# RWKV's key slabs and low-rank output slab: split beside three feed-forward output products instead of at the passage into RWKV, in a hybrid Mamba-2/RWKV-7 trunk on one Trainium2 core

## The chip, the core and the metric

The kernel runs on one core of one Trainium2 chip. The metric is the device time of one execution in microseconds (us); lower is better. The engines have these names in the rows: PE is TensorE's matrix multiply, PEld its weight load, DVE is VectorE, ACT is ScalarE, POOL is GpSimd, SP is SyncE, which here issues nearly all DMAs (SPq is its queue). The timeline counts microseconds from the start of the profiled span.

## The reference, cut to what matters

512 frames of 1024 features run through two layers. Each layer is feed-forward, mixer, feed-forward; the first mixer is a Mamba-2 scan, the second RWKV-7. All arrays are float32.

```python
def swiglu_ffn(x, w_in, w_out):
    gate, up = jnp.split(x @ w_in, 2, axis=-1)
    return (jax.nn.silu(gate) * up) @ w_out
...
def rwkv7_mixer(u, v_first, mix, w_rkv, w_o, w0, w1, w2, a0, a1, a2, g1, g2, ...):
    delta = jnp.pad(u, ((0, 0), (1, 0), (0, 0)))[:, :-1] - u
    shift = lambda idx: u + delta * mix[idx]
    r, k, v = shift(0) @ w_rkv[0], shift(2) @ w_rkv[1], shift(3) @ w_rkv[2]
    w_log = -softplus(-(w0 + jnp.tanh(shift(1) @ w1) @ w2)) - 0.5
    alpha = jax.nn.sigmoid(a0 + (shift(4) @ a1) @ a2)
    ...                                    # recurrence over frames, group norm, gate
    return (y * g) @ w_o, v

def reference(x, norms, ffn_w_in, ffn_w_out, ...):
    for i in range(2):
        t = swiglu_ffn(rmsnorm(h, norms[i, 0]), ffn_w_in[i, 0], ffn_w_out[i, 0])
        h = h + 0.5 * rmsnorm(t, norms[i, 1])
        u = rmsnorm(h, norms[i, 2])
        t = mamba2_mixer(u, ...) if i == 0 else rwkv7_mixer(u, ...)
        h = h + rmsnorm(t, norms[i, 3])
        t = swiglu_ffn(rmsnorm(h, norms[i, 4]), ffn_w_in[i, 1], ffn_w_out[i, 1])
        h = h + 0.5 * rmsnorm(t, norms[i, 5])
    return h
```

## The kernel before, in words

**Three products for one.** Every float32 matrix product is made of three passes on PE. A weight slab, 128 x 1024 floats (512 KB), is loaded into a tile `raw`; ACT casts it to a high part (`whi`, line 112), DVE or POOL subtracts that from the original to get the low part (`wlo`, line 113). Activations are split likewise: `hh`, `hl` for the hidden tiles of a feed-forward block, `xmh`, `xml` for RWKV's mixed inputs. `mm3` then multiplies high by high, high by low and low by high.

**The stream.** The class `Stream` numbers all weight slabs of the program in the order of their use and loads and splits them ahead of it. There are four `raw` buffers and eight buffers each for `whi` and `wlo`. `get()` hands out the next slab and prefetches; `pause_after` and `resume` stop and restart it. All loads go through SP's queue, in one order; an entry that has no free buffer holds up everything behind it.

**Kept slabs.** Some slabs of RWKV are loaded and split long before they are used. Their two parts are stored in DRAM (`khi_d`, `klo_d`, line 150) and later loaded as parts straight into `whi` and `wlo` (line 126), so that no engine splits them then. `Stream.store` is a generator: each step loads one such slab, splits it (always on DVE) and sends off the parts of the one before. The feed-forward blocks step it (`more`) beside their output products. Before, 16 slabs are kept: RWKV's eight r slabs and eight v slabs.

**The stages.** They are `ffn0`, `mamba`, `ffn1`, `ffn2`, `rwkv`, `ffn3`. Each ends in `out_phase`, which multiplies by the output weights: for a feed-forward block 22 slabs, one for each hidden tile k (`acc` banks). Up to k = 17 (k = 13 in `ffn2`) PE takes slab after slab; the rest is multiplied half by half of the frames, so that the norm of the first half can start. There a scheduler sets the order of the instructions of all engines from the program's order; from the tail on the order of ACT, DVE and POOL is that of the code.

**The passage from `ffn2` into `rwkv`.** The last eight output slabs are held in all eight buffers and multiplied half by half (`deep`). As the last of them end, the norm of the second half (`nb`), the mixing of RWKV's inputs (`xa`, `xb`) and the first products of the keys (`nxt.pair`, banks `pk`) are interleaved by a string of letters, run by `run`. `0`, `1`, `2` each multiply one k of a pair of heads (six matmuls); `x` and `y` mix one k of the first or second half; `N` and `n` step the norm; `e` and `z` square and scale the last bank; `s` and `t` split the next slab, `s` with its low part on DVE, `t` on POOL. The strings are `S0`, `S1` and `SEQ`. In this part the order on PE is that of the code, too.

Of the kernel before, what the change touches and what calls it, by code (L numbers as in the profile page):

```python
# [57 lines left out]
SQ = 8  # L58

S0 = "ttxxx"  # L60
S1 = "xxt"
SEQ = "s00ezN1x11NN10x110nxN00n0111222tt22NNx02x"

# [7 lines left out]
def step(g, n=1):  # L73
    for _ in range(n):
        next(g, None)


class Stream:
# [5 lines left out]
    def __init__(self, nc, raw, split, dram, aps, stored, own, ahead=6, split_ahead=4):  # L84
        self.nc, self.raw, self.split, self.aps, self.own = nc, raw, split, aps, own
        self.kept = {i: [dram.tile([P, SLAB], F32, tag=f"{z}{i}", name=f"{z}_d") for z in ("khi", "klo")]
                     for i in range(stored[0], stored[0] + stored[1])}
        self.loaded, self.parts = [], []
        self.pos = 0
        self.lo_eng = nc.vector  # L90
        self.ahead, self.split_ahead = ahead, split_ahead
        self.limit = len(aps)
        self.hold = False
# [42 lines left out]
    def store(self, first, n):  # L136

        made = None
        for i in list(self.kept)[first:first + n]:
            t = self._raw(i)  # L140
            if made:
                self._send(*made)
            made = i, self._parts(i, *t, self.nc.vector)
            yield
        self._send(*made)
        yield
# [25 lines left out]
    def get(self):  # L172
        i = self.pos
        self.pos += 1
        self.prefetch(i)
        return self.parts[i]
# [81 lines left out]
class Trunk:  # L258
    def __init__(self, ctx, tc, ins, out, plan=("ffn0", "mamba", "ffn1", "ffn2", "rwkv", "ffn3")):
        nc = self.nc = tc.nc  # L260
        self.tc, self.ins = tc, ins
        self.const = ctx.enter_context(tc.tile_pool(name="const", bufs=1))
        self.small = ctx.enter_context(tc.tile_pool(name="small", bufs=4))
        self.ps = ctx.enter_context(tc.tile_pool(name="ps", bufs=8, space=PSUM))
        self.dram = ctx.enter_context(tc.tile_pool(name="dram", bufs=1, space=DRAM))
        raw = ctx.enter_context(tc.tile_pool(name="raw", bufs=4))
        split = ctx.enter_context(tc.tile_pool(name="split", bufs=8))
        self.slots = ctx.enter_context(tc.tile_pool(name="slots", bufs=54))

        make = {"ffn": Ffn, "mam": Mamba, "rwk": Rwkv}  # L270
        gis = {"ffn0": 0, "mamba": 2, "ffn1": 4, "ffn2": 6, "rwkv": 8, "ffn3": 10}
        stages = [make[p[:3]](self, gis[p], 0.5 if p[0] == "f" else 1.0) for p in plan]
        slabs = [s.slabs() for s in stages]
        base = [sum(map(len, slabs[:i])) for i in range(len(plan))]
        own = set()
        for b, s in zip(base, stages):
            s.base = b
            own |= {b + i for i in s.own()}
        self.stream = Stream(nc, raw, split, self.dram, [ap for z in slabs for ap in z],
                             (base[plan.index("rwkv")] + 9, 16), own)  # L280

        self.h = [self.slot("h") for _ in range(KD)]
        x = ins["x"].rearrange("p (k t) -> p k t", k=KD)
        self.vec = self.const.tile([P, V_END], F32, tag="vec", name="vec")
        self.cst = self.const.tile([P, C_END], F32, tag="cst", name="cst")
        nc.scalar.dma_start(self.vec[:, :V_CW], ins["vec"][:, :V_CW])
        for hf in range(2):
            self.stream.load_ahead(hf + 1)
            for k in range(KD):
                nc.sync.dma_start(self.h[k][:, HALF[hf]], x[:, k, HALF[hf]])  # L290
        self.stream.load_ahead(4)
        nc.sync.dma_start(self.cst, ins["cst"])
        nc.sync.dma_start(self.vec[:, V_CW:], ins["vec"][:, V_CW:])
        self.ident = self.cst[:, C_ID:C_ID + P]
        self.ones = self.cst[:, C_ONE:C_ONE + P]
        self.tri = self.cst[:, C_TRI:C_TRI + P]

        self.fill = iter(())
        self.new_rs()
        first = stages[0]  # L300
        first.start()
        for i, st in enumerate(stages):
            st.body(stages[i + 1] if i + 1 < len(stages) else Output(self, out))
# [104 lines left out]
    def out_phase(self, get, nk, gi, scale, nxt, side=None, wide=False, eps=None, more=iter(())):  # L408
# [7 lines left out]
        nc = self.nc  # L416
# [33 lines left out]
        def mm(hf, m, k, w, x):  # L450
            c = cols(m, k)
            self.mm3(place[hf, m], [a[:, c] for a in w], [a[:, HALF[hf]] for a in x],
                     k == 0 and (hf, m // 2) in pairs and m % 2 == 0, k == nk - 1)

        def mm_all(m, k, w, x):
            c = cols(m, k)
            self.mm3(banks[m], [a[:, c] for a in w], x, k == 0, k == nk - 1)
# [6 lines left out]
        for k in range(nk):  # L464
            if deep and k == nk - tail:
                self.stream.pause_after(tail)
            if not deep or k < nk - tail:
                ws.append(slab(k))
            xs.append(get(k))
            if k < nk - tail:  # L470
                for m in range(2 * len(mps)):
                    if whole:
                        mm_all(m, k, ws[-1], xs[-1])
                    else:
                        for hf in range(2):
                            mm(hf, m, k, ws[-1], xs[-1])
                step(side)
                if k % 2:
                    step(more)
            elif one_half:  # L480
                for m in range(KD):
                    mm(0, m, k, ws[-1], xs[-1])
                    step(side)
# [24 lines left out]
        def squared(hf, mp, sq=None):  # L508
            if sq is None:
                sq = self.slot("sq")  # L510
                if (hf, mp) in pairs:
                    nc.scalar.square(sq, pairs[hf, mp])
                else:
                    for m in (2 * mp, 2 * mp + 1):
                        square(sq, hf, m)
            eng = nc.vector if mp == 3 else nc.gpsimd
            if mp:
                self.tt(sq, sqs[hf], sq, ALU.add, eng)
            if mp == 3:
                self.tt(sq[:, HALF[0]], sq[:, HALF[0]], sq[:, HALF[1]], ALU.add)  # L520
            sqs[hf] = sq

        def scaled(hf, mp):

            for m in (2 * mp, 2 * mp + 1):
                scale_tile(hf, m)
# [39 lines left out]
        def run(ops):  # L566


            for i in ops:
                if i == "e":  # L570
                    squared(1, 3)
                elif i == "z":
                    scaled(1, 3)
                elif i in "012":
                    nxt.pair(int(i))
                elif i in "st":
                    self.stream.lo_eng = nc.vector if i == "s" else nc.gpsimd
                    self.stream.parts_ahead(len(self.stream.parts) - self.stream.pos + 1)
                    self.stream.lo_eng = nc.vector
                else:  # L580
                    if i == "N":
                        self.fill = xa
                    step({"x": xa, "y": xb, "q": pb}.get(i, nb))
                    self.fill = iter(())

        with self.tc.manual_schedule(engines=ORDERED):
# [21 lines left out]
            else:  # L608
# [24 lines left out]
                for mp in range(4):  # L633
                    if deep:
                        for i in range(2):
                            ks = nk - tail + 4 * i
                            across(1, (mp,), range(ks, ks + 4))
                            if mp == 3 and i == 0:
                                run(S1)
                            step(na, (1, 6, 0, 0, 1, 0, 0, 0)[2 * mp + i])  # L640
# [12 lines left out]
            if deep:  # L653
                with self.tc.manual_schedule(engines=ORDERED | {mybir.EngineType.PE}):
                    run(SEQ)
                    for i in range((nxt.HEAD + nxt.MORE) // 2):
# [59 lines left out]
class Ffn(Stage):  # L716
# [157 lines left out]

    def store(self):

        first, n = {0: (0, 6), 4: (6, 5), 6: (11, 5)}.get(self.gi, (0, 0))
        return self.t.stream.store(first, n) if n else iter(())

    def eps_out(self):  # L880
# [1199 lines left out]
```

## Time and profile before

| | |
|---|---|
| three runs | 2415.03, 2415.22, 2416.76 us; median 2415.22 |
| profiled execution | 2416.49 us, its span 2414.8 us, mean granted clock 0.982 |
| busy share of the span | PE 95%, PEld 86%, DVE 72%, ACT 45%, POOL 15% |
| chain of work that ended last | PE 71%, DVE 16%, ACT 5%, DMA 3% |
| DMA | 331.82 MB, mean 137 GB/s; HBM read 270.82 MB, written 58.33 MB |
| loads of kept parts (`khi_d`, `klo_d` each) | 16, first at 1651.0 us |
| stores of kept parts | from 256.9 to 1497.9 us |

How to read it: busy shares are means over stages that have different limits. A row of a timeline gives start, length, engine, line, operation, output and inputs, shapes and count; in brackets stands the idle time of the engine before it and the engine that ended it. A row of slices gives the stretch, its length, the busy time of PE, PEld, DVE, ACT and POOL with their instruction counts, TensorE's granted clock (1.00 is full), the mean busy share of the DMA engines and GB/s. The output products begin near 246 us (`ffn0`), 1085 us (`ffn1`) and 1447 us (`ffn2`); the passage into RWKV runs from 1570 to 1620 us.

### The profile page before, as it was taken

To read this page: it belongs to the slowest core of one execution; us is meant where nothing else is said; L and a number is where in the kernel's file an instruction comes from. 1 tells how busy PE (TensorE), PEld (TensorE's weight loads), DVE (VectorE), ACT (ScalarE), POOL (GpSimd) and SP (SyncE) were. 2 spreads that over 40 slices of the span, in tenths; PEclk is the share of its full clock that TensorE was granted. 3 is DMA by queue.
4 is the path that set the end of the run, shared out by engine and by line. 5 is a ranking of instruction groups with operands and counts; after the bars stand their busy time and mean duration, and the time that the engine had idled before them with its cause. 6 is when DMAs were issued, how large, how long until landed. Compare 5 with 4: busy or idle time off the path is not lost.

```text
span 2414.8 us, 40973 instructions
## 1 busy us (share of the span) xinstructions
PE 2304.1 (95%) x16232; PEld 2087.8 (86%) x16232; DVE 1737.1 (72%) x3002; ACT 1097.2 (45%) x1765; POOL 373.5 (15%) x335
## 2 busy tenths in 40 slices
PE   8999998899999999999999999979898999999998
PEld 7999787678887989998889999976677898899987
DVE  6888548988886578875489875476783567888843
ACT  5544433454543244444245444256743343554531
POOL 1000003323222110000020000162422333000001
PEclk9999999899999999999999999989998999999999
DMA  4333841444334223349214339225764322233531
GB/s 151 125 131 131 304 156 62 144 129 147 124 133 147 80 78 133 132 137 323 90 40 145 132 137 316 80 92 180 237 213 119 88 66 97 83 123 131 187 141 36
DMA packets 156672, 331.82 MB, mean 137 GB/s; under 512 B 35456, under 2 KB 62464, under 8 KB 156480
## 3 DMA queue, kind: packets, MB, share of 16 engines
q1 hardware_dynamic: 155760, 328.63, 40.0%
q8 instruction: 127, 2.08, 0.4%
q10 hardware_dynamic: 720, 0.57, 0.1%
q14 instruction: 65, 0.53, 0.1%
HBM read 270.82 MB, written 58.33 MB: 136 GB/s over the span
## 4 chain that ended last, share of the span: by engine, by line
PE 71%; DVE 16%; ACT 5%; DMA 3%; issue 2%; POOL 1%; SPq 0%; DVEq 0%; ACTq 0%; POOLq 0%
PE acc L313 22%; PE one L313 16%; PE two L313 11%; PE pj L313 7%; PE xy L313 2%; DVE wlo L113 2%; PE gram L313 1%; PE pk L313 1%; PE gu L313 1%; PE head L313 1%; DVE row L1171 1%; PE y L313 1%; DVE conv L332 1%; PE rs_bank L313 1%; DVE xl L332 1%
## 5 line engine op out<-in xcount | busy, mean ns | idle before, releaser
L113 DVE TENSOR_TENSOR wlo<-raw,whi 128x1024 fp32r<-128x1024 f32 x218 | 270.8, 1259 | 217.2 <-ACT whi L112 206.6
L313 PE MATMUL acc<-hl,whi 128*128 128x256 f32 (+1 forms) x1168 | 384.7, 330 | 2.7 <-DVE hl L325 2.5
L313 PE MATMUL acc<-hh,whi 128*128 128x256 f32 (+1 forms) x1168 | 383.4, 330 | 4.1 <-ACT hh L324 4.1
L313 PE MATMUL acc<-hh,wlo 128*128 128x256 f32 (+1 forms) x1168 | 383.6, 329 | 0.0
L112 ACT CAST whi<-raw 128x1024 fp32r<-128x1024 f32 x228 | 232.7, 1044 | 284.8 <-PE acc L313 109.1
L329 POOL TENSOR_TENSOR sq<-sq 128x256 f32<-128x256 f32 (+1 forms) x67 | 70.7, 1055 | 1455.1 <-ACT sq L506 1042.5
L313 PEld LDWEIGHTS acc<-hl,whi 128*128 128x128 f32 x1168 | 222.5, 190 | 24.8 <-DVE hl L325 5.3
L313 PEld LDWEIGHTS acc<-hh,whi 128*128 128x128 f32 x1168 | 221.9, 191 | 24.6 <-ACT hh L324 5.4
L313 PEld LDWEIGHTS acc<-hh,wlo 128*128 128x128 f32 x1168 | 222.4, 190 | 19.4
L313 PE MATMUL one<-hh,whi 128*128 128x256 f32 x816 | 232.1, 284 | 2.2 <-DVE diff L329 2.1
L313 PE MATMUL one<-hl,whi 128*128 128x256 f32 x816 | 231.4, 284 | 0.0
L313 PE MATMUL one<-hh,wlo 128*128 128x256 f32 x816 | 231.4, 284 | 0.0
L329 DVE TENSOR_TENSOR wlo<-raw,whi 128x1024 fp32r<-128x1024 f32 (+1 forms) x136 | 129.3, 955 | 68.5 <-ACT whi L912 67.6
L329 DVE TENSOR_TENSOR wlo<-sums,whi 128x1024 fp32r<-128x1024 f32 x136 | 160.3, 1217 | 0.0
L313 PEld LDWEIGHTS one<-hh,whi 128*128 128x128 f32 x816 | 157.1, 193 | 3.5 <-DVE diff L329 2.9
L313 PEld LDWEIGHTS one<-hl,whi 128*128 128x128 f32 x816 | 157.2, 193 | 0.0
L313 PEld LDWEIGHTS one<-hh,wlo 128*128 128x128 f32 x816 | 157.2, 193 | 0.0
L313 PE MATMUL two<-xh,whi 128*128 128x256 f32 x544 | 154.2, 283 | 0.0
L313 PE MATMUL two<-xl,whi 128*128 128x256 f32 x544 | 154.2, 283 | 0.0
L313 PE MATMUL two<-xh,wlo 128*128 128x256 f32 x544 | 154.1, 283 | 0.0
L313 PE MATMUL pj<-xh,whi 128*128 128x512 f32 x360 | 147.8, 410 | 0.0
L313 PE MATMUL pj<-xl,whi 128*128 128x512 f32 x360 | 142.4, 396 | 0.0
(366 smaller groups left out, 6049.4 us busy)
## 6 DMA issues: line engine op xcount, KB each, us to landing
raw<-in_win_dram SPq DMA_DIRECT2D x176, 512.0 KB, 4.2
raw<-in_wout_dram SPq DMA_DIRECT2D x88, 512.0 KB, 5.5
raw<-in_min_dram SPq DMA_DIRECT2D x48, 512.0 KB, 3.3
hid_d<-hid SPq DMA_DIRECT2D x72, 256.0 KB, 2.2
hid<-hid_d SPq DMA_DIRECT2D x72, 256.0 KB, 5.6
row<-mrows SPq DMA_DIRECT2D x64, 256.0 KB, 6.1
raw<-in_rkrv_dram SPq DMA_DIRECT2D x24, 512.0 KB, 6.0
khi_d<-whi SPq DMA_DIRECT2D x16, 512.0 KB, 3.3
```

The costliest lines, as they stand in the source:

```text
L112: self.nc.scalar.copy(hi[:, :n], t[:, :n])
L113: eng.tensor_tensor(out=lo[:, :n], in0=t[:, :n], in1=hi[:, :n].bitcast(F32), op=ALU.subtract)
L313: self.nc.tensor.matmul(out, lhsT, rhs, start=start, stop=stop, skip_group_check=True)
L329: (eng or self.nc.vector).tensor_tensor(out=out, in0=a, in1=b, op=op)
L332: self.nc.vector.scalar_tensor_tensor(out=out, in0=a, scalar=s, in1=b, op0=op0, op1=op1)
L1171: nc.vector.tensor_scalar(out=r[:, c * P:(c + 1) * P], in0=r[:, c * P:(c + 1) * P], scalar1=acum3[:, c, h:h + 1], scalar2=0.0, op0=ALU.sub ...
```

## The change: what it does

RWKV's eight key slabs and the slab `w2a2` of its low-rank outputs join the kept ones: 25 slabs instead of 16. `ffn0` stores nine (keys and `w2a2`), `ffn1` nine (r and one of v), `ffn2` seven (v), instead of 6, 5 and 5; since nine slabs take ten steps, `more` is stepped at k = 0 as well. In the strings, `t` loads the next slab's two parts from DRAM; `s` and the choice of POOL go. Eight `t` stand in the strings instead of six splits and two within `2`.

```diff
-S1 = "xxt"
-SEQ = "s00ezN1x11NN10x110nxN00n0111222tt22NNx02x"
+S1 = "xxtt"
+SEQ = "tt00ezN1x11NN10x110nxN00n0111tt22222NNx02x"
...
-                             (base[plan.index("rwkv")] + 9, 16), own)
+                             (base[plan.index("rwkv")], 25), own)
...
                 step(side)
-                if k % 2:
+                if k % 2 or k == 0:
                     step(more)
...
-                elif i in "st":
-                    self.stream.lo_eng = nc.vector if i == "s" else nc.gpsimd
+                elif i == "t":
                     self.stream.parts_ahead(len(self.stream.parts) - self.stream.pos + 1)
-                    self.stream.lo_eng = nc.vector
...
-        first, n = {0: (0, 6), 4: (6, 5), 6: (11, 5)}.get(self.gi, (0, 0))
+        first, n = {0: (0, 9), 4: (9, 9), 6: (18, 7)}.get(self.gi, (0, 0))
```

The order of the instructions changes in two places. First, ACT at the start of `ffn0`'s output products (`ffn1` and `ffn2` have the same pattern). `whi` and `raw` carry the slab's number: 44 to 65 are the output slabs, 263 and up are RWKV's; the `hh` of the hidden tiles k = 1, 2, 3, 4 read `hid_555`, `hid_2814`, `hid_2858` and `hid_2897`. Before:

```order
L324 CAST hh_2945<-hid_555 128x512
L112 CAST whi48_2970<-raw48_2924 128x1024
L112 CAST whi49_3000<-raw49_2966 128x1024
L967 ACTIVATE side_2783<-side_2783 128x512
L324 CAST hh_3042<-hid_2814 128x512
L112 CAST whi272_3030<-raw272_3028 128x1024
L112 CAST whi50_3036<-raw50_2968 128x1024
L112 CAST whi51_3072<-raw51_2998 128x1024
L324 CAST hh_3078<-hid_2858 128x512
L112 CAST whi273_3110<-raw273_3106 128x1024
L112 CAST whi52_3116<-raw52_3034 128x1024
L324 CAST hh_3122<-hid_2897 128x512
```

The same stretch now, where k = 2, 3, 4 read `hid_2832`, `hid_2876` and `hid_2915`:

```order
L112 CAST whi48_2988<-raw48_2942 128x1024
L965 ACTIVATE side_2801<-side_2801 128x512
L324 CAST hh_3068<-hid_2832 128x512
L112 CAST whi263_3018<-raw263_3016 128x1024
L112 CAST whi49_3024<-raw49_2984 128x1024
L324 CAST hh_3104<-hid_2876 128x512
L112 CAST whi264_3056<-raw264_3052 128x1024
L112 CAST whi50_3062<-raw50_2986 128x1024
L112 CAST whi51_3098<-raw51_3022 128x1024
L112 CAST whi265_3136<-raw265_3132 128x1024
L112 CAST whi52_3142<-raw52_3060 128x1024
L324 CAST hh_3148<-hid_2915 128x512
```

Three casts of kept slabs stand ahead of the tile of k = 4 instead of two. SP's queue at the same place, before:

```order
L104 DMA raw51_2998<-in_wout_dram 128x1024
L104 DMA raw272_3028<-in_rkrv_dram 128x1024
L104 DMA raw52_3034<-in_wout_dram 128x1024
L811 DMA hid_3040<-hid_d_482 128x512
L811 DMA hid_3076<-hid_d_482 128x512
L150 DMA khi_d_75<-whi272_3030 128x1024
L104 DMA raw53_3070<-in_wout_dram 128x1024
L104 DMA raw273_3106<-in_rkrv_dram 128x1024
L150 DMA klo_d_76<-wlo272_3031 128x1024
L104 DMA raw54_3114<-in_wout_dram 128x1024
```

And now:

```order
L104 DMA raw263_3016<-in_rkrv_dram 128x1024
L104 DMA raw51_3022<-in_wout_dram 128x1024
L809 DMA hid_3066<-hid_d_500 128x512
L809 DMA hid_3102<-hid_d_500 128x512
L150 DMA khi_d_75<-whi263_3018 128x1024
L104 DMA raw264_3052<-in_rkrv_dram 128x1024
L150 DMA klo_d_76<-wlo263_3019 128x1024
L104 DMA raw52_3060<-in_wout_dram 128x1024
L150 DMA khi_d_77<-whi264_3056 128x1024
L104 DMA raw53_3096<-in_wout_dram 128x1024
L104 DMA raw265_3132<-in_rkrv_dram 128x1024
```

The first kept slab's load has moved ahead of output slab 51, and a second round, with its load and two stores, stands ahead of slabs 52 and 53. The second place is the passage into RWKV. ACT there, with key slabs 265 and 266, before:

```order
L1351 ACTIVATE xm_16361<-u_16300,om_16140 128x256
L1339 CAST xmh_16354<-xm_16353 128x256
L112 CAST whi265_16368<-raw265_16284 128x1024
L112 CAST whi266_16398<-raw266_16286 128x1024
L512 ACTIVATE sq_16416<-acc13_14894 128x512
```

And now:

```order
L1337 CAST xmh_16404<-xm_16403 128x256
L1349 ACTIVATE xm_16443<-u_16382,om_16230 128x256
L1337 CAST xmh_16436<-xm_16435 128x256
L512 ACTIVATE sq_16506<-acc13_14968 128x512
L1349 ACTIVATE xm_16525<-u_16383,om_16230 128x256
```

The square of the last bank follows the mixing directly. On SP's queue, instead of eight loads of key slabs around the first stores of h (`rh`), there now stand 16 loads of parts behind them (the first eight of them):

```order
L1325 DMA rh_16229<-h_131 128x256
L126 DMA whi263_16370<-khi_d_75 128x1024
L126 DMA wlo263_16371<-klo_d_76 128x1024
L126 DMA whi264_16374<-khi_d_77 128x1024
L126 DMA wlo264_16375<-klo_d_78 128x1024
L126 DMA whi265_16450<-khi_d_79 128x1024
L126 DMA wlo265_16451<-klo_d_80 128x1024
L126 DMA whi266_16454<-khi_d_81 128x1024
L126 DMA wlo266_16455<-klo_d_82 128x1024
```

Of these, 263 and 264 belong to the first pair of heads (`0`), 265 and 266 to the second (`1`); four more slabs follow in the same way, then the stores of h for the second half.

## The prediction

> **What bounds the kernel now.** I read the page first, then the stages that the change touches, in slices of time and as a timeline of each engine.
>
> ```profile
> span 2414.8 us, 40973 instructions
> PE 2304.1 (95%) x16232; PEld 2087.8 (86%) x16232; DVE 1737.1 (72%) x3002; ACT 1097.2 (45%) x1765; POOL 373.5 (15%) x335
> ```
>
> TensorE is busy for 95% of the span, so time can come only out of the 110.7 us in which it waits, or out of stretches in which its clock is low; and anything that makes it wait anew is paid in full. The stage with the thickest gap is the one the change aims at, the passage from the third feed-forward block into RWKV (each row: stretch, length, busy PE, PEld, DVE, ACT, POOL, granted clock, DMA share, GB/s).
>
> ```profile
> 1570.00:1580.00 10.00, 8.26 (x68) 7.94 (x67) 7.54 (x13) 5.93 (x11) 8.16 (x6) 1.00 0.24 75
> 1580.00:1590.00 10.00, 5.02 (x23) 4.72 (x24) 7.11 (x17) 4.22 (x8) 4.24 (x4) 0.51 0.42 135
> 1590.00:1600.00 10.00, 9.56 (x75) 9.00 (x74) 9.83 (x16) 8.06 (x17) 8.20 (x9) 0.98 0.33 108
> 1600.00:1610.00 10.00, 6.29 (x49) 6.01 (x50) 8.32 (x16) 0.00 (x0) 4.54 (x2) 1.00 0.66 215
> 1610.00:1620.00 10.00, 7.37 (x49) 6.98 (x48) 8.01 (x17) 7.18 (x17) 6.32 (x8) 0.83 0.07 23
> ```
>
> PE is busy for 36.5 of these 50 us: 13.5 us are idle. The timeline of PE names what ended the larger waits (start, length, ..., in brackets the idle time before and its releaser):
>
> ```profile
> 1586.10 1.01 PE L313 MATMUL rs_bank<-cst,sq 128*128 128x1 f32 x4 [4.98 <-DVE sq L329]
> 1602.35 0.39 PE L313 MATMUL pk<-xmh,wlo 128*128 128x256 f32 x1 [2.67 <-DVE wlo L113]
> 1607.34 0.83 PE L313 MATMUL rs_bank<-cst,sq 128*128 128x1 f32 x6 [1.01 <-DVE sq L329]
> 1613.66 0.38 PE L313 MATMUL pk<-xmh,whi 128*128 128x256 f32 x1 [2.07 <-ACT xmh L1339]
> ```
>
> Three of the four stand behind weight splits: the DVE work they wait for is queued behind these rows, which cost more here than elsewhere, because POOL subtracts at the same time.
>
> ```profile
> L113 DVE TENSOR_TENSOR wlo<-raw,whi 128x1024 fp32r<-128x1024 f32 x217 | 270.4, 1263 | 213.7 <-ACT whi L112 203.0 <-DMA klo_d<-wlo 9.5 <-issue 0.7
> 1582.45 2.53 DVE L113 TENSOR_TENSOR wlo<-raw,whi 128x1024 fp32r<-128x1024 f32 x1 [2.36 <-ACT whi L112]
> 1597.24 5.06 DVE L113 TENSOR_TENSOR wlo<-raw,whi 128x1024 fp32r<-128x1024 f32 x2
> 1602.22 5.06 DVE L329 TENSOR_TENSOR sq<-sq 128x256 f32<-128x256 f32 x6
> ```
>
> **What is removed.** Eight key slabs lose their cast on ACT and their subtraction here (three on DVE, 2.53 + 5.06 = 7.6 us; five on POOL). The ninth split, of the low-rank slab, stood beside the key products, where PE never waits, so it is worth nothing:
>
> ```profile
> 1614.60 18.75 PE pk L313 x143
> ```
>
> **What is put in their place at the passage.** SP issues 16 loads of 512 KB, a high and a low part for each slab. They can't start early: the eight buffers of each kind hold the last eight output slabs, and the first is given back at 1572.00, where before the first cast waited for it.
>
> ```profile
> 1572.00 2.00 ACT L112 CAST whi<-raw 128x1024 fp32r<-128x1024 f32 x2 [0.39 <-PE acc L313]
> L126 SPq DMA_DIRECT2D whi<-khi_d x16: 382/472/677, 1651.0 to 1768.8; - x16
> DMA to landing us min/median/max: 3.2/4.4/9.3
> GB/s 240 23 0 113 150 41 221 0 0 262 0 229 229 332 369 406 430 410 385 94 8 0 262 295 207 336 190 324 360 383 389 416 246 25 0 0 151 349 25 0
> ```
>
> The first lands 3.2 us after 1572.0. The others follow at what the DMA engines move: 430 GB/s at best in the slices of the last row (1.22 us for 512 KB), 315 in the mixed traffic of the feed-forward stage (row below; 1.66 us). I take 1.45 us, the middle: the eighth part, with which the second pair of heads can be multiplied, lands at 1575.2 + 7 x 1.45 = 1585.4. Before, PE came to that pair at 1587.0, when the sums that started at 1586.10 were done. So 1.6 us are gained there, not the whole 5 us: the wait for the splits is replaced by one for the loads. After that nothing is late any more: the 2.67 us behind the low part and the 1.01 us behind the squares go, since DVE has 7.6 us less to do and runs without POOL beside it. The 2.07 us behind the mixed inputs stay, as does the low clock. Gain 1.6 + 2.7 + 1.0 = 5.3 us; PE is full from 1614.60 on (row above), so it reaches the end. Ends: with 1.22 us a part 6.9 us; with 1.66 us 3.8 us; nothing, if parts land 9.3 us after issue like the worst.
>
> Behind the 16 loads on SP's queue stand the stores of h and the constants, and then four more pairs of parts ahead of the key stores:
>
> ```profile
> 1594.95 4.00 SPq L1327 DMA_DIRECT2D rh<-h  x8
> 1637.88 13.02 SPq L1476 DMA_DIRECT2D rk<-k  x6
> ```
>
> The 16 issues need 16 x 0.47 = 7.5 us and the last buffer is free when the output products end, near 1577, so SP is through by 1580, 15 us before h is to be stored. The four pairs wait for buffers of the keys, which are given back when their products end, at 1633.35 (1614.60 + 18.75), 4.5 us before the key stores: 8 x 0.47 = 3.8 us. Both cost nothing, the second with 0.7 us to spare.
>
> **What is added in the three feed-forward blocks.** Nine more slabs are cast and subtracted there. ACT (9 x 1.0 us) and DVE (9 x 1.26 us) have room; the traffic is 9 x 1.5 MB more, in a stage that already moves 315 GB/s:
>
> ```profile
> 260.00:270.00 10.00, 8.96 (x39) 6.82 (x38) 4.29 (x6) 3.98 (x5) 0.00 (x0) 1.00 0.95 315
> ```
>
> PE's one gap in that stage shows what matters. ACT works in order: the cast of a stored slab waits for its load, and behind it stand the cast of the hidden tile that PE needs next and, on DVE, its low part.
>
> ```profile
> 248.85 0.33 SPq L104 DMA_DIRECT2D raw<-in_wout_dram  x1
> 252.58 0.33 SPq L104 DMA_DIRECT2D raw<-in_rkrv_dram  x1
> 255.87 2.95 ACT L112 CAST whi<-raw 128x1024 fp32r<-128x1024 f32 x3 [3.06 <-DMA raw<-in_rkrv_dram]
> 259.34 0.33 SPq L104 DMA_DIRECT2D raw<-in_rkrv_dram  x1
> 265.68 2.00 ACT L112 CAST whi<-raw 128x1024 fp32r<-128x1024 f32 x2 [6.34 <-DMA raw<-in_rkrv_dram]
> 267.58 0.61 ACT L324 CAST hh<-hid 128x512 fp32r<-128x512 f32 x1
> 269.04 0.68 DVE L325 TENSOR_TENSOR hl<-hid,hh 128x512 fp32r<-128x512 f32 x1
> 269.78 0.50 PE L313 MATMUL acc<-hl,whi 128*128 128x512 f32 x1 [0.80 <-DVE hl L325]
> ```
>
> The casts of two stored slabs stand ahead of the fifth hidden tile (267.58), and PE already comes 0.8 us too soon for it. In the new order three stand ahead of it (order below the change), because of the extra step at the first slab. Each round is a load, its cast and subtraction, and only then the next load: 255.87 to 259.34 is 3.5 us. The new first load takes the queue place of the output slab at 248.85. Loads took 3.3 us (252.58 to 255.87) or 6.3 us (259.34 to 265.68); for the first two, with less traffic around them, I take 4.8, the middle, and for the third 6.3, since the same transfers stand around it as around the second before. Cast and subtraction of the first take 1.0 + 1.26 = 2.3 us. So: 248.85 + 4.8 + 2.3 + 4.8 + 3.5 + 6.3 = 270.6, against 265.68: the tile is 4.9 us late, and PE waits 4.9 us longer. With all three at 3.3 us it would come at 264.5, 1.2 us early and no loss; with all at 6.3, at 273.6, 8.0 us late. All three blocks have the same rows, the same waits, and no slack:
>
> ```profile
> ACT whi L112 <- DMA raw<-in_rkrv_dram: 9.4, 2, 6.3
> ACT whi L112 <- DMA raw<-in_rkrv_dram: 9.3, 2, 6.2
> ACT whi L112 <- DMA raw<-in_rkrv_dram: 8.9, 2, 6.1
> PE acc L313 <- DVE hl L325: 0.3, 1, 0.3
> ```
>
> (First, second and third block; the last row is PE's wait in the third.) So 3 x 4.9 = 14.7 us. Nothing is caught up later, as PE is full behind it:
>
> ```profile
> 290.00:300.00 10.00, 10.00 (x46) 8.28 (x45) 4.67 (x6) 3.96 (x6) 0.00 (x0) 1.00 0.92 316
> 330.00:340.00 10.00, 10.00 (x46) 8.29 (x45) 1.65 (x2) 1.05 (x1) 0.00 (x0) 1.00 0.30 104
> 269.15 0.33 SPq L104 DMA_DIRECT2D raw<-in_rkrv_dram  x1
> ```
>
> The rounds after these last about 9.8 us (259.34 to 269.15), less than the 10.4 us that PE takes for two slabs (48 matmuls at 46 in 10 us), so no second stall follows. The last stores end later than before, up to the last slab ahead of PE's tail, where DMA had room (0.30 from 330 us on): no cost, unless the next stage's first slabs come late.
>
> **The clock after a stall.** A stall of 0.8 + 4.9 us is longer than the one of 4.98 us above, behind which the clock was low:
>
> ```profile
> 1586.00:1590.00 4.00, 3.90 (x18) 3.90 (x19) 3.51 (x14) 1.30 (x3) 0.52 (x1) 0.50 0.60 190
> 1590.00:1594.00 4.00, 4.00 (x33) 3.84 (x33) 3.93 (x9) 2.89 (x7) 2.35 (x4) 0.96 0.02 6
> ```
>
> 4 us at 0.50 and 4 at 0.96 are 2.2 us of lost work; I take 2.1 each, 6.3 us for three. After the idle 2.67 us at 1602 the clock stayed at 1.00, so a stall half as long would cost nothing here: ends 0 and 6.5.
>
> The Trainium skill, page "TensorE: Matmul & The Clock Gate", section "Part 1: The HAM clock gate (the "warmup" mystery)", gives a window of about 3.4 us, idle until the clock halves and busy until it is back. By it a stall would cost an estimated 1.7 us, and the sum would be 1.2 us lower; the rows show a little over 4 us at half rate, and I keep them.
>
> **Sum.** +14.7 + 6.3 - 5.3 = +15.7 us. The profiled execution took 2416.5 us (span 2414.8); the median of the runs, 2415.2, is 1.3 lower. 2415.2 + 15.7 = 2430.9: 2431 us.
>
> **The rivals.** *The extra round is hidden (faster).* If the first three loads each land in 3.3 us, the hidden tile is in time and PE gains only: 2415.2 - 5.3 = 2410, at best 2408. It decides from a third load that is cast no later than 0.5 us after 265.68. For it: the first load of before did land in 3.3. Against: DMA is 0.95 busy here and the second took 6.3. *Short stalls (no change).* Each about 2 us, without the low clock: 3 x 2 - 5.3 = +0.7, 2416. It needs loads near 3.8 us. *The passage gains nothing.* The 16 loads land late, or what follows waits for them: +21, 2436. Against: DMA is at 0.24 to 0.42 there.
>
> **How the numbers follow.** Forecast 0.58 (its own range 2421 to 2440: stalls of 2.9 to 6.9 us, gain of 3.8 to 6.9), passage without gain 0.10, no change 0.18, faster 0.14. A measurement of this kernel can tell about 0.2%, 4.8 us: below 2410.4 is faster, above 2420.0 slower. So faster 0.14, same 0.18, slower 0.68. The range 2410 to 2440 leaves out about half of the faster case and the worst stalls.
>
> **What would show it.** Right: PE waits 5 to 6 us for hl once in each of the first three blocks, some 20 us after the output products begin, with the clock near 0.5 behind it; the third cast of a stored slab there starts near 270.6; the passage has no wlo on DVE or POOL, and PE's second pair starts near 1585 when counted from the last output product of before. Wrong, if that hl wait stays under 2 us (then the loads were quick), or if the passage shrinks by 10 us (then the loads kept ahead of PE).

## The result and the profile after

| | before | after |
|---|---|---|
| median of six runs | 2416.84 us | 2431.14 us |
| lowest and highest | 2415.03, 2420.13 | 2425.73, 2436.82 |
| profiled execution, its span | 2416.5, 2414.8 | 2431.34, 2429.6 |
| mean granted clock | 0.982 | 0.977 |

The changed kernel takes 1.0062 times as long (95% interval 1.0048 to 1.0075), which is 15.0 us on 2415. Times here are medians of all runs; one of the twelve runs of experiment 1 took 5218.34 us, at a granted clock of 1.00, for a reason that no trace shows, and is left out of its ratio. The first lines of the changed kernel's page:

```profile
span 2429.6 us, 41054 instructions
PE 2309.8 (95%) x16232; PEld 2091.9 (86%) x16232; DVE 1736.3 (71%) x3007; ACT 1097.4 (45%) x1765; POOL 357.5 (15%) x330
```

PE has the same 16232 matmuls. Its busy time grew by 5.7 us (2304.1 to 2309.8), which, as the matmuls are the same, I read as a lower clock, and its idle time by 9.1 us (110.7 to 119.8). The timeline of PE shows where the new idle time stands; in brackets the wait and what ended it:

```profile
273.74 1.65 PE L313 MATMUL acc<-hh,whi 128*128 128x512 f32 x3 [5.66 <-ACT hh L324]
1120.63 1.65 PE L313 MATMUL acc<-hh,whi 128*128 128x512 f32 x3 [5.22 <-ACT hh L324]
1491.20 2.08 PE L313 MATMUL acc<-hh,whi 128*128 128x256 f32 x8 [4.48 <-ACT hh L324]
```

There is one such wait in each of the first three feed-forward blocks, where before PE waited 0.2 + 0.8, 0.8 and 0.3 us. The loads and casts of stored slabs in front of the first wait, and the cast that it waits for, picked out of the rows of SP and ACT in order of time:

```profile
248.95 0.33 SPq L104 DMA_DIRECT2D raw<-in_rkrv_dram  x1
253.18 2.00 ACT L112 CAST whi<-raw 128x1024 fp32r<-128x1024 f32 x2 [0.43 <-DMA raw<-in_rkrv_dram]
255.53 0.33 SPq L104 DMA_DIRECT2D raw<-in_rkrv_dram  x1
262.00 2.96 ACT L112 CAST whi<-raw 128x1024 fp32r<-128x1024 f32 x3 [6.30 <-DMA raw<-in_rkrv_dram]
265.47 0.33 SPq L104 DMA_DIRECT2D raw<-in_rkrv_dram  x1
271.18 1.99 ACT L112 CAST whi<-raw 128x1024 fp32r<-128x1024 f32 x2 [6.22 <-DMA raw<-in_rkrv_dram]
273.07 0.61 ACT L324 CAST hh<-hid 128x512 fp32r<-128x512 f32 x1
```

Three loads of stored slabs, three casts that wait for them, and behind the third the cast of the fifth hidden tile, which PE has been waiting for since 268.08. SP had issued the load of that hidden tile by 242.77; ACT was idle for 6.22 us in front of it, because the instruction ahead of it in its queue had no data. Behind each of the three waits the clock is low (slices; clock, DMA share and GB/s are the last three numbers):

```profile
273.70:281.00 7.30, 7.26 (x24) 5.51 (x25) 3.25 (x4) 1.46 (x2) 0.00 (x0) 0.77 0.89 276
1120.60:1128.00 7.40, 7.37 (x19) 5.43 (x20) 3.25 (x4) 1.75 (x3) 0.00 (x0) 0.57 0.86 290
1491.20:1499.00 7.80, 7.80 (x48) 7.80 (x49) 3.21 (x4) 1.42 (x2) 0.00 (x0) 0.71 0.81 279
```

Work lost there: 7.30 x 0.23 + 7.40 x 0.43 + 7.80 x 0.29 = 7.1 us.

At the passage into RWKV the waits behind the splits are gone. What PE waited for, in total, number of times and longest, from the end of the output products to the wait of 2.1 us that stays; before:

```profile
PE rs_bank L313 <- DVE sq L329: 6.3, 3, 5.0
PE pk L313 <- DVE wlo L113: 2.7, 1, 2.7
PE pk L313 <- ACT xmh L1339: 2.1, 1, 2.1
PE pk L313 <- POOL xml L329: 1.7, 1, 1.7
```

After:

```profile
PE pk L313 <- ACT xmh L1337: 2.1, 1, 2.1
PE pk L313 <- DMA wlo<-klo_d: 2.0, 3, 0.8
PE pk L313 <- DMA whi<-khi_d: 1.5, 2, 0.8
```

So 10.7 us of waits for DVE and POOL went, and 3.5 us of waits for the part loads came. The slices in which they stand, and the last of the 16 load issues on SP:

```profile
1600.00:1604.00 4.00, 2.41 (x18) 1.96 (x16) 2.05 (x5) 0.57 (x1) 0.68 (x2) 1.00 1.01 410
1604.00:1608.00 4.00, 2.03 (x7) 1.29 (x6) 3.79 (x15) 1.90 (x5) 0.96 (x2) 0.61 1.04 422
```
```profile
1594.81 0.32 SPq L126 DMA_DIRECT2D whi<-khi_d  x1
...
1606.25 0.32 SPq L126 DMA_DIRECT2D whi<-khi_d  x1
1607.52 0.32 SPq L126 DMA_DIRECT2D wlo<-klo_d  x1
```

The DMA engines are full (share 1.01 and 1.04, 410 and 422 GB/s), and a part moves every 1.27 us: here they set PE's pace. The place of the program in time is read from rows that both kernels have. These are some of the changed kernel:

```profile
72.68 0.39 PE L313 MATMUL one<-xh,wlo 128*128 128x256 f32 x1 [2.20 <-DVE wlo L329]
383.91 0.60 PE L313 MATMUL rs_bank<-cst,sq 128*128 128x1 f32 x4 [1.31 <-DVE sq L329]
920.21 0.39 PE L313 MATMUL one<-xh,wlo 128*128 128x256 f32 x1 [2.25 <-DVE wlo L329]
1289.49 0.39 PE L313 MATMUL one<-xh,wlo 128*128 128x256 f32 x1 [2.24 <-DVE wlo L329]
1628.72 0.55 PE L313 MATMUL pk<-xmh,whi 128*128 128x256 f32 x1 [2.07 <-ACT xmh L1337]
```

With the same rows of the other profiled executions, the length of each stretch in us (`ffn1` from the third row to the fourth; Mamba ends at its own wait for `hh`, at 765.62 here, and the last stretch at the wait of 2.25 us ahead of `ffn3`, at 2118.99 here; the versions are those of the experiments below):

| stretch | before | after | step removed | before + step | two steps | step at the end |
|---|---|---|---|---|---|---|
| `ffn0` | 305.41 | 311.23 | 305.68 | 310.37 | 316.17 | 303.76 |
| Mamba | 377.67 | 381.71 | 373.59 | 378.53 | 376.32 | 378.64 |
| `ffn1` | 364.45 | 369.28 | 362.25 | 370.02 | 373.90 | 360.54 |
| `ffn2` and passage | 339.60 | 339.23 | 332.23 | 345.72 | 345.13 | 331.60 |
| RWKV to `ffn3` | 491.49 | 490.27 | 489.58 | 490.49 | 492.64 | 494.24 |

The changed kernel loses 5.8 us in `ffn0` and 4.8 in `ffn1`; in the fourth stretch a stall of the same kind and the gain at the passage cancel. Mamba differs by 4.0 us, too, but no instruction of it was changed, and over the six executions of the table it takes 373.6 to 381.7 us in no order that follows the edits. With the same 2005 matmuls, PE was busy 2.4 us longer (352.5 before, 354.9 after) and idle 1.7 us longer. That is scatter of single executions; I did not find its source.

### The profile page after: what moved, and what is told of

It reads as the page before. It is cut to its first block, busy times and chain, and to the rows that moved or that the text cites. A ratio compares the mean times of both kernels' runs of the same rounds, so it can differ in the third digit from the quotient of the medians.

```text
span 2429.6 us, 41054 instructions
## 1 busy us (share of the span) xinstructions
PE 2309.8 (95%) x16232; PEld 2091.9 (86%) x16232; DVE 1736.3 (71%) x3007; ACT 1097.4 (45%) x1765; POOL 357.5 (15%) x330
## 4 chain that ended last, share of the span: by engine, by line
PE 72%; DVE 13%; ACT 5%; DMA 4%; issue 2%; POOL 1%; SPq 0%; DVEq 0%; ACTq 0%; POOLq 0%
PE acc L313 22%; PE one L313 15%; PE two L313 11%; PE pj L313 8%; PE xy L313 2%; PE pk L313 2%; DVE wlo L113 1%; PE gram L313 1%; DMA raw<-in_wout_dram 1%; PE gu L313 1%; PE head L313 1%; PE y L313 1%; DVE row L1169 1%; PE rs_bank L313 1%; ACT xf L817 1%
```

## The experiments

Theory A: the extra step at the first slab puts a third cast that waits for a load ahead of the fifth hidden tile on ACT, and this costs the time; the passage itself gains. Rival B: it is the traffic and the work of nine more slabs, wherever they stand. Times are medians; a ratio is to the kernel before, run on the same chip between them, with its 95% interval.

**1. The step removed from the change.** All 25 slabs are still kept.

```diff
-                if k % 2 or k == 0:
+                if k % 2:
                     step(more)
...
         for _ in side:
             pass
+        for _ in more:
+            pass
         order.close()
```

> All 25 slabs are still split early and kept; only the extra step at the first slab is gone, and the last store is made behind the loop. Theory A (the cost is the third stored cast ahead of the fifth hidden tile): the three waits of PE for hh fall from 5.7, 5.2 and 4.5 us to about 1 us or less, the clock stays at 1.00 behind them, the passage keeps its gain, and the time is 2413 us (2408 to 2417), below the kernel before. Rival B (the cost is the traffic and the work of nine more slabs, wherever their steps stand): 2426 to 2433 us, with the idle time spread over the blocks.

Measured: 2413.13 us, ratio 0.9978 (0.9964 to 0.9992). What PE waited for among the output products of `ffn0` and of `ffn1`:

```profile
PE acc L313 <- DVE hl L325: 1.6, 2, 0.8
PE acc L313 <- DVE hl L325: 1.0, 2, 0.8
```

The waits for `hh` are gone, and the version is faster than the kernel before. By the table the three blocks give back 5.6, 7.0 and 7.0 us against the changed kernel, and the passage keeps its gain: 7.4 us less than before in the fourth stretch. B is out.

**2. The step alone, in the kernel before.** The same 16 slabs as before; only the condition becomes `if k % 2 or k == 0:`.

> The kernel before with the extra step alone: the same 16 slabs, three stored casts ahead of the fifth hidden tile. Theory A: a wait of 4 to 6 us for hh in each of the three blocks, 18 us in all with the clock (5.8, 4.9 and 7.4 us by the offsets of the two traces): 2434 us (2429 to 2438). Rival B: 2415 to 2420 us, since not one slab more is split.

Measured: 2435.32 us, ratio 1.0080 (1.0068 to 1.0092). PE's waits in the three blocks, in order:

```profile
PE acc L313 <- ACT hh L324: 4.8, 1, 4.8
PE acc L313 <- ACT hh L324: 6.3, 1, 6.3
PE acc L313 <- ACT hh L324: 4.1, 1, 4.1
```

The step costs 19.3 us (0.80%) with not one slab more split, as the theory had it. The ratios of the two halves of the change, 1.0080 and 0.9978, multiply to 1.0058; the whole has 1.0062.

**3. One tile's cast moved ahead.** The changed kernel with its step, but the parts of the fifth hidden tile are made with those of the fourth.

```diff
         self.fetch(k + 4)
-        return self.first[k] if k < len(self.first) else self.t.parts(self.hid.pop(k))
+        if len(self.first) <= k:
+            self.first.append(self.t.parts(self.hid.pop(k)))
+        if k == 3:
+            self.first.append(self.t.parts(self.hid.pop(4)))
+        return self.first[k]
```

> The changed kernel with its extra step, but the parts of the fifth hidden tile are made together with those of the fourth, so that two stored casts stand ahead of it and not three; loads, splits and stores are the same. Theory A: the waits for that tile fall to 1.5 us or less, 2415 us (2410 to 2420). Rival B: 2426 to 2433 us. A third way, that the sixth tile now waits in its place: 2420 to 2430 us with waits of 2 to 4 us five microseconds later.

Measured: 2422.33 us, ratio 1.0025 (1.0015 to 1.0036): by the ratios 9 us less than the changed kernel, where 16 were expected. The third way came about, two tiles later rather than one:

```profile
284.51 3.35 PE L313 MATMUL acc<-hh,whi 128*128 128x512 f32 x7 [2.88 <-ACT hh L324]
1125.65 1.89 PE L313 MATMUL acc<-hh,whi 128*128 128x512 f32 x7 [2.00 <-ACT hh L324]
1491.20 1.21 PE L313 MATMUL acc<-hh,whi 128*128 128x256 f32 x8 [1.46 <-ACT hh L324]
```

The tile that was moved no longer waits, with loads, splits and stores as before; it is the order on ACT. But the chain of stored slabs runs late from its start, and the seventh tile now stands behind the fourth cast of it, which started at 281.00.

**4. A second extra step.** The changed kernel with `if k % 2 or k in (0, 2):`, so four stored casts ahead of the fifth tile.

> The changed kernel with a second extra step, at the third slab: four stored casts ahead of the fifth hidden tile. Theory A: one more round of load, cast, subtraction and next load, 8 to 10 us by the distance of the second and the third cast (262.00 to 271.18), is added to each of the three waits: 13 to 15 us each, 2455 to 2462 us. Rival B, or a queue that lets the loads run ahead: 2428 to 2437 us.

Measured: 2444.22 us, ratio 1.0113 (1.0100 to 1.0127), with waits of 9.2, 9.8 and 9.9 us. More steps cost more, as A says, but a further one costs 12 us by the ratios, not the 24 to 31 expected. The casts on ACT show the wrong size:

```profile
251.89 2.00 ACT L112 CAST whi<-raw 128x1024 fp32r<-128x1024 f32 x2 [0.27 <-DMA raw<-in_rkrv_dram]
260.50 2.00 ACT L112 CAST whi<-raw 128x1024 fp32r<-128x1024 f32 x2 [6.09 <-DMA raw<-in_rkrv_dram]
266.95 1.99 ACT L112 CAST whi<-raw 128x1024 fp32r<-128x1024 f32 x2 [4.45 <-PE acc L313]
273.55 1.99 ACT L112 CAST whi<-raw 128x1024 fp32r<-128x1024 f32 x2 [4.61 <-DMA raw<-in_rkrv_dram]
```

From the second to the third group and from the third to the fourth it is 6.45 and 6.6 us. (The row of the third names PE as what it waited for last, so its time need not be the load's alone.) The 9.2 us from which I had taken the price of a round lie between the step at k = 1 and the one at k = 3, with the casts of two output slabs between them; a step at k = 2 divides that distance, 13.05 in place of 9.2, and adds 3.9 us. Measured were 3.5, 4.6 and 5.4 us more of waiting.

**5. The extra step at another place.** All 25 slabs and an extra step, as in the change; the stores begin at k = 3 and the extra step stands two slabs ahead of the tail. From version 1:

```diff
-                if k % 2:
+                if (k % 2 and k > 1) or k == nk - tail - 2:
                     step(more)
```

> All 25 slabs as in the change, with an extra step as in the change, but that step stands two output slabs ahead of the end and the stores begin at the fourth slab. Theory A (it is the place of the extra step that costs, not its being there, nor the number of slabs): no wait for hh over 1 us, 2404 to 2410 us, 21 to 27 us below the changed kernel. Rival B (the three slabs more, or the step wherever it stands): 2413 us and more.

Measured: 2406.03 us, ratio 0.9955 (0.9939 to 0.9971): 0.45% below the kernel before. On ACT the cast of the fifth tile is now the second of the pair of `hh`, ahead of the first stored slab:

```profile
256.62 1.14 ACT L324 CAST hh<-hid 128x512 fp32r<-128x512 f32 x2
263.44 2.96 ACT L112 CAST whi<-raw 128x1024 fp32r<-128x1024 f32 x3 [5.68 <-DMA raw<-in_rkrv_dram]
```

No wait of PE for `hh` or `hl` is left among the output products of the three blocks. In the three blocks the nine more slabs cost nothing that can be seen; the place of the step was the price. (Behind the passage they bring a wait of 1.6 us here, which the section on the prediction explains.) It is the lowest ratio of all versions, with 6, 8 and 9 inside its interval.

**6. Late start with 22 slabs.** From version 1, `if k % 2 and k > 1:`, so 8, 8 and 6 slabs are stored and the last three of v are split where they are used.

> As the version without the extra step (2413 us), with the stores begun at the fourth output slab; so 22 slabs are kept and the last three of the values are split where they are used, as all others that are not kept. Theory A: the waits of 0.8 us left in the blocks go and nothing else changes: 2409 to 2412 us. Rival: the three values split late cost DVE or a wait in RWKV's products: 2413 to 2418 us.

Measured: 2406.73 us, ratio 0.9963 (0.9950 to 0.9976), by the ratios 3.6 us under version 1; 1 to 4 were expected, though the time itself came out below the range. The waits for `hl` that the kernel before already had are gone; by the same rows as above the three stretches shrink by 2.0, 1.5 and 1.3 us against version 1, so theory A holds here, too, and splitting three values late costs nothing that can be seen.

**7. Four key slabs split at the passage.** From version 1, the kept slabs begin at the fifth key slab (21 slabs, seven in each block).

```diff
-                             (base[plan.index("rwkv")], 25), own)
+                             (base[plan.index("rwkv")] + 4, 21), own)
```

> As the version without the extra step (2413 us), but the first four key slabs are not kept: they are loaded early as they are and split in the passage, so that 8 part loads are left there and not 16; 21 slabs are stored, 7 in each block. Theory P (the passage is now bound by the part loads at what the DMA engines move): PE's waits for parts (0.87, 0.78, 0.78, 0.90 and 0.49 us in that version) and the low clock behind them go, 2404 to 2410 us. Rival Q (it is the splits on DVE that bind it, and four of them bring back a wait for wlo or for sq of 2 to 5 us): 2411 to 2418 us.

Measured: 2414.66 us, ratio 0.9989 (0.9975 to 1.0004), near version 1, with Q's wait. The waits for parts went, and the old one came back:

```profile
1582.10 1.01 PE L313 MATMUL rs_bank<-cst,sq 128*128 128x1 f32 x4 [4.27 <-DVE sq L329]
```

Four casts on ACT and four subtractions on DVE stand in their queues ahead of the squares of the last bank, the last two of each directly (casts from 1577.55, the square at 1579.45; subtractions from 1578.63, the sums of squares at 1580.90). That is enough to make PE wait 4.27 us. So P and Q both hold in part: parts bind the passage through DMA, splits bind it through ACT and DVE. Each of these subtractions took 1.18 us; the one of 2.53 us before, at 1582.45, had POOL subtracting beside it until 1583.90.

**8. The same with the late start** (8, 7 and 6 slabs).

> As the version with four key slabs kept, but the stores begin at the fourth output slab, so that no stored cast stands ahead of the fifth hidden tile (8, 7 and 6 slabs in the three blocks). Theory A: the waits of 0.8 us for the low part that are left in the blocks go, 1 to 4 us less than that version: 2402 to 2409 us if P holds there, 2408 to 2416 if Q holds. Rival B: no change against that version.

Measured: 2407.24 us, ratio 0.9967 (0.9955 to 0.9979), by the ratios 5.3 us under version 7, where 1 to 4 were expected (the intervals allow it). No wait for `hh` or `hl` is left in the blocks; 4.26 us stay at the passage.

**9. Six key slabs kept.** The version of 6, with the 22 kept slabs moved on by two.

> As the version with the late start (2406.7 us, 22 slabs), with the window of kept slabs moved on by two: the first two key slabs are split in the passage, 12 part loads are left there. If the waits for the part loads (about 3.6 us) and the wait for sq behind the splits (4.3 us with four splits, none with none) both shrink in proportion, the passage gains 1 to 3 us: 2403 to 2406 us. Rival: two splits already bring the wait for sq back, 2407 to 2411 us.

Measured: 2405.95 us, ratio 0.9960 (0.9947 to 0.9974), against 0.9963 for 6: no difference that can be told, where a gain of 1 to 3 us was expected. The trade is real but even: the fourth stretch takes 330.96 us here and 330.95 in version 6. The five waits for parts are gone, and this one is back:

```profile
1577.36 0.97 PE L313 MATMUL rs_bank<-cst,sq 128*128 128x1 f32 x4 [1.71 <-DVE sq L329]
```

## Why the prediction was right, term by term

**The stalls, +14.7 us.** Right in place, cause and size. The third cast of a stored slab started at 271.18; 270.6 was predicted. The waits sum to 15.4 us, against 2.1 before: 13.3 us. Three details were off. PE waited for `hh`, not for `hl` as I wrote: with the tile so late the high part is missing first. The three load times came as 4.2, 6.5 and 5.7 us, where I had taken 4.8, 4.8 and 6.3; the sum fits by compensation. And the round is not a fixed time, as experiment 4 shows.

**The clock, +6.3 us.** 7.1 us by the slices. Together the two terms were predicted at 21.0 us; the three blocks give back 19.6 us when the step goes (experiment 1), and the step alone costs 19.3 us (experiment 2). My further remark that a stall half as long costs nothing is not borne out: it rested on one row, and the last section shows that this row stands alone. The ends of the forecast's own range, 2421 and 2440, do not follow exactly from its terms either: with stalls of 2.9 us, the clock at 6.3 and a gain of 6.9 they give 2423.3, with 6.9, 6.5 and 3.8 they give 2438.6. Nothing hangs on this.

**The passage, -5.3 us.** The mechanism was right, the size too small: from the last output product (1576.84 before, 1599.65 after) to the end of the wait that stays (1613.66 and 1628.72) it is 36.8 us before and 29.1 after, 7.7 us less, above my upper end of 6.9. The term that failed is the 1.6 us for the second pair of heads. I let it start with the eighth part. The eighth part did come about as predicted: PE got it at 1607.50, 7.9 us after the last output product, and 8.6 was predicted. But PE did not wait for it as a whole:

```profile
1603.68 0.36 PE L313 MATMUL pk<-xmh,whi 128*128 128x256 f32 x1
1604.94 0.58 PE L313 MATMUL pk<-xmh,wlo 128*128 128x256 f32 x1 [0.78 <-DMA wlo<-klo_d]
1606.22 0.58 PE L313 MATMUL pk<-xmh,whi 128*128 128x256 f32 x1 [0.70 <-DMA whi<-khi_d]
1607.50 0.58 PE L313 MATMUL pk<-xmh,wlo 128*128 128x256 f32 x1 [0.49 <-DMA wlo<-klo_d]
```

The pair began 4.0 us after the last output product and took each part as it landed. Counted to the end of its first six matmuls, the pair gained 3.3 us and not 1.6: the next matmul started 11.56 us after the last output product before (1588.40) and 8.23 us after it now (1607.88). The 1.7 us that PE had waited for POOL's `xml` went with the splits, too; that wait stood ahead of the one for the squares and is within these 3.3 us. The waits that I priced at 2.7 and 1.0 us went as said; with smaller ones the rest of the gain is 4.4 us. A part took 1.27 us, near the 1.22 of my lower end, not 1.45.

**The costs put at nothing.** One of them was not: the four pairs of parts that SP issues ahead of the key stores, to which I had given 0.7 us to spare. They fill the DMA engines just when the keys are stored (1652 to 1656 us: clock, DMA share, GB/s), ACT waits for a store to land before it can cast the next mixed input, and PE waits for what stands behind that on ACT:

```profile
1652.00:1656.00 4.00, 4.00 (x19) 3.30 (x18) 1.50 (x3) 3.03 (x6) 0.00 (x0) 1.00 1.00 396
```
```profile
1663.22 0.62 ACT L1337 CAST xmh<-xm 128x512 fp32r<-128x512 f32 x1 [2.84 <-DMA rk<-k]
1664.96 1.03 PE L313 MATMUL kacc<-sq,rc 128*12 128x512 f32 x2 [1.70 <-ACT sq L1473]
```

Before, the DMA share was 0.33 when the key stores began (1637 to 1641 us). The wait of 1.70 us (1.4 to 2.5) stands in all nine versions that keep keys and in neither of the two that don't. I had counted the issues on the queue, not the transfers, nor that a cast on ACT waits for the store. No run took it away alone, so its price, 1.7 us, is read from the trace only. The others did cost nothing: SP was through with the 16 parts at 1607.8, 5 us later than forecast but ahead of the stores of h at 1612.71; no second stall followed in the blocks; and nine more splits are hidden, as experiment 5 shows.

**The sum.** +15.7 us predicted, +15.0 by the ratio. The terms as measured in the one profiled execution make 13.3 + 7.1 - 7.7 + 1.7 = +14.4, its difference to the one before is 14.8. That this is so close is luck, as three differences of these two executions are not in it. Mamba took 4.0 us more. In `ffn1` the stall (4.4) and the clock behind it (3.2) make 7.6 us, but the stretch grew by 4.8 only, since the kernel before had lost 3.4 us to a low clock at its start (last section). And from RWKV to `ffn3`, which is 1.2 us shorter with the wait of 1.7 us in it, 2.9 us came back, among others where the clock, low for a while behind the wait for `r` in both, was 0.79 in 40 us before and 0.89 after.

**The rivals.** The hidden round needed a third cast by 266.2; it came at 271.18. The passage without gain is refuted by experiment 1. No change needed short loads of 3.8 us; they took 4.2 to 6.5.

## What to carry to other kernels

Work that is put beside a busy stage is free only if none of its waits stands in an in-order queue ahead of what the bounding engine needs next: count, at the first use, how many instructions with a late input stand ahead of it. Where such a step is put can decide the sign: the same 25 slabs cost 0.62% with the extra step at the front of the loop and gain 0.45% with it near the end and the first step later. When loads replace computation, price the first products by the landing of the parts that they read, one by one.

## What the hardware showed that was not expected

After the same wait, the clock can be low or not. The wait of 2.25 us for a low part ahead of `ffn1` stands at 909.61 us before and at 920.21 us after; the slices behind it, of before and of after:

```profile
909.60:914.00 4.40, 3.83 (x21) 3.56 (x22) 4.40 (x6) 1.05 (x3) 0.00 (x0) 0.67 0.73 272
914.00:918.00 4.00, 4.00 (x21) 4.00 (x20) 3.29 (x6) 3.22 (x6) 0.00 (x0) 0.51 0.07 28
```
```profile
920.20:924.20 4.00, 3.35 (x25) 3.15 (x26) 4.00 (x6) 1.15 (x4) 0.00 (x0) 1.00 0.75 267
924.20:928.20 4.00, 3.92 (x33) 3.72 (x32) 3.97 (x7) 3.83 (x6) 0.00 (x0) 1.00 0.17 63
```

Before, some 3.4 us were lost to it (4.40 x 0.33 + 4.00 x 0.49); after, none. In the second place of this kind it was the other way round (1.00 before, 0.67 after). The same wait (2.2 us) stands ahead of `ffn1`, `ffn2` and `ffn3` in all eleven traces, and the clock in the 4 us behind it is low (0.57 to 0.69) in one, seven and five of the eleven. Waits of 2.9, 2.0 and 1.5 us in experiment 3 were followed by 0.57, 1.00 and 0.71. Longer waits leave little to chance: the eleven traces have 79 waits of PE of 2.6 us and more behind its first matmul, and 78 of them are followed by a clock of 0.50 to 0.79 over 4 us. The one exception is the wait of 2.67 us at 1602.35 of the kernel before, the row from which the prediction took it that a stall half as long costs nothing. (PE's first wait of the program, 6.1 to 6.7 us, is followed by 1.00 in all eleven.) The Trainium skill, page "TensorE: Matmul & The Clock Gate", section "Part 1: The HAM clock gate (the "warmup" mystery)", says that the window of about 3.4 us runs freely and is not started by the program, so that the number of slow matmuls varies from run to run. The rows agree as to the variation; with that page's idle window of about 3.4 us alone the low clock behind 2.25 us would not come, though in the 4.60 us that end with it PE was busy for only 2.35. The scatter of the runs, 11 us over six runs of the changed kernel, may come from this; that was not tested.
